# Three couples of tiles in seven products, for the last four attention pairs of layer A

## The chip, the cores and the metric

One Trainium2 chip, and one core of it. The metric is device time of one launch in microseconds; the median of three runs of the kernel before is 2052.78 us (2052.01 to 2052.95).

## What is computed

Two transformer layers over 256 rows of width 2048, in float32. The change touches the first sublayer of layer A, its attention with a combined projection to queries, keys, values and a forget gate:

```
u = rms_norm(h, a_norm_g[l])
proj = u @ a_w_in[l]
q, k, v, fz = jnp.split(proj, [D, 2 * D, 3 * D], axis=-1)
q = rms_norm(q.reshape(B, S, H, Dh), a_q_g[l])
k = rms_norm(k.reshape(B, S, H, Dh), a_k_g[l])
...
o = forgetting_attention(q, k, v, logf)
h = h + o.reshape(B, S, D) @ a_w_out[l]
h = h + sq_relu_mlp(h, mlp_norm_g[layer], mlp_w1[layer], mlp_w2[layer])
```

The rest is an MLP of width 8192, a shared key and value projection, a second attention with a query projection of its own, and a second MLP. All the matrices are 2048 deep or 2048 wide; their float32 weights are read from HBM once, some tiles twice.

## The kernel before

**Products.** A product of 256 rows with a weight is cut into panels of 512 output columns. The rows are two blocks of 128, and the depth is 16 tiles of 128. A *unit* is a weight tile of 128 partitions by 1024 columns: two depth tiles of one panel. Each float32 operand is split in two parts, `hi` (rounded to the format that TensorE multiplies fast) and `lo` (the rest), and a product is three passes: hi times hi (L592), lo of the activations (L594) and lo of the weights (L596). A plain unit is 2 depth tiles x 2 row blocks x 3 passes = 12 matmuls of 512 columns.

**Splitting.** `issue` (L305) takes the next unit: ScalarE (ACT) writes `hi` (L323), VectorE (DVE) subtracts to get `lo` (L324). There are three buffers for each, and `top_up` (L340) keeps up to three units ready ahead of TensorE (PE). `load` (L289) brings plain units into four `raw` buffers from the queue of SyncE (SP), three units ahead (`EARLY`).

**Seven products.** Panels are taken in *pairs* (class `Pair`). Of a pair, the first depth tiles of both panels are multiplied by the scheme of Strassen in Winograd's form: a couple of row blocks, two depth halves and two panels make eight block products, of which seven are needed. One *couple* is such a square of 2 depth tiles x 2 panels. The weights of a pair come as four blocks "11", "12", "21", "22" (`bring`, L921), and the weight side needs the sums T3 = 22 + 12, T2 = T3 + 11, T1 = 12 + 11 and T4 = 21 + T2 (the minus signs lie with the activations), of which T3 and T2 are added by DVE (`make`, L944), and T1 and T4 by an accumulating DMA from GpSimd's (POOL's) queue (`put`, L972), which reads the block a second time. The seven weight operands are called *forms* (11, T3, T2, T1, 21, T4, 22). The activation side needs sums of the row blocks (`sums`, L386; tiles `S`). In the attention of layer A a pair takes two couples: blocks of 128x1024, seven forms of 2 x 3 = 6 matmuls, then six plain units for each of the two panels. In the MLPs a pair takes four couples (`DEEP`), each block 128x2048 and each form split in two halves.

**Order of the work.** Everything on SP, ACT, DVE and PE runs in the order in which Python wrote it (`keep_order`, L88). `plan_heads` (L261) makes the list of units for the attention of layer A: one pair with the panels of (v0, q1), and four more with (k1, v1), (q2, k2), (v2, q3), (k3, v3). `TABLES["ORD"]` interleaves the forms with plain units; the six numbers of `HF` and `HS` say how many plain units before a pair's first form each block is brought or summed (`prepare`, L982). The steps of attention (softmax, norms, transposes) stand in a queue `fill`; `run` (L998) takes as many of them after each unit as the table `HM` says.

**Space.** Blocks lie in the right halves of the four rooms `k0`, `k1`, `v0`, `v1` (`sub`), whose left halves hold normed keys and values; T3 and T2 lie in a tile of the pool `acts`. Query tiles use the tags `q` and `s` (`scale_q`, L692), two buffers of each. `h` holds the residual rows; they are read in at the start and first changed by the output projection.

## Time and profile before

| | |
|---|---|
| median of three runs | 2052.78 us |
| the profiled execution's own time | 2049.66 us |
| its span (first to last instruction) | 2047.9 us |
| granted TensorE clock | 0.999 |
| PE busy | 2041.1 us, 9062 records |
| DVE busy | 1783.5 us |
| ACT busy | 1403.7 us |
| POOL busy | 245.0 us |
| data moved by DMA | 557.78 MB |

"Busy" is the time in which an engine has at least one instruction under way. PE's instructions overlap (a matmul lasts longer than the distance to the next one), so the distance between starts is what a matmul costs. The four attention pairs that the change concerns lie from about 86 us to about 270 us of the span.

### The profile page before, as it was taken

What the parts mean: (1) busy time and instruction counts of PE and PEld (TensorE: products, weight loads), DVE (VectorE), ACT (ScalarE), POOL (GpSimd) and SP (SyncE); (2) the same over time, 40 slices, a digit from 0 to 9 for tenths busy, and PEclk for the clock granted to TensorE, in tenths of its full rate; (3) what the DMA queues carried; (4) which work ended last, traced back from release to release, by engine and by line L of the source; (5) the groups of instructions that cost most, each with busy time, mean ns of one, the idle gap of its engine ahead of it and who ended that gap; (6) DMA issues with size and microseconds to landing.
All of it is one profiled execution on the core that took longest, in us unless ns stands there. A gap on an engine that the chain in (4) does not pass through costs nothing.

```text
span 2047.9 us, 27097 instructions
## 1 busy us (share of the span) xinstructions
PE 2041.1 (100%) x9062; PEld 1688.5 (82%) x9062; DVE 1783.5 (87%) x2065; ACT 1403.7 (69%) x1805; POOL 245.0 (12%) x351
## 2 busy tenths in 40 slices
PE   9999999999999999999999999999999999999999
PEld 7888888888888888888888888888888888888887
DVE  7788888998898899899988778888988998988996
ACT  7766666677677677677778666667766676776764
POOL 1111110011111102101012111001101111111020
PEclk9999999999999999999999999999999999999999
DMA  8898888998888898898879888888988888888984
GB/s 322 265 298 272 266 280 243 309 278 272 282 262 281 272 293 272 247 292 273 260 242 311 275 254 287 255 264 284 291 291 265 266 270 284 266 284 261 299 259 147
DMA packets 175309, 557.78 MB, mean 272 GB/s; under 512 B 40624, under 2 KB 69184, under 8 KB 152640
## 3 DMA queue, kind: packets, MB, share of 16 engines
q1 hardware_dynamic: 154112, 464.99, 63.9%
q0 software_dynamic: 20768, 90.75, 22.5%
q8 instruction: 71, 1.16, 0.2%
q14 instruction: 70, 0.57, 0.1%
q10 hardware_dynamic: 288, 0.30, 0.1%
HBM read 516.07 MB, written 27.29 MB: 265 GB/s over the span
## 4 chain that ended last, share of the span: by engine, by line
PE 98%; DVE 1%; ACT 1%; issue 0%; DMA 0%; DVEq 0%; ACTq 0%
PE acc L596 23%; PE acc L592 23%; PE acc L594 23%; PE s L592 9%; PE s L594 9%; PE s L596 9%; PE po L729 1%; PE po L766 1%; DVE lo L324 0%; PE po L767 0%; PE po L728 0%; ACT hi L323 0%; DMA gsb<-in_gs 0%; PE pg L868 0%; DVE s L995 0%
## 5 line engine op out<-in xcount | busy, mean ns | idle before, releaser
L324 DVE TENSOR_TENSOR lo<-raw,hi 128x1024 fp32r<-128x1024 f32 (+1 forms) x409 | 493.5, 1211 | 81.5 <-ACT hi L323 77.1
L323 ACT ACTIVATE hi<-raw 128x1024 fp32r<-128x1024 f32 (+1 forms) x409 | 429.5, 1054 | 194.0 <-PE acc L594 123.4
L592 PE MATMUL acc<-hi,act 128*128 128x512 f32 x1774 | 496.3, 393 | 0.7 <-ACT hi L323 0.7
L596 PE MATMUL acc<-lo,act 128*128 128x512 f32 x1774 | 491.1, 390 | 0.7 <-DVE lo L324 0.6
L594 PE MATMUL acc<-hi,act 128*128 128x512 f32 x1774 | 490.7, 389 | 0.0
L596 PEld LDWEIGHTS acc<-lo,act 128*128 128x128 f32 x1774 | 332.5, 188 | 72.1 <-DVE lo L324 3.1
L594 PEld LDWEIGHTS acc<-hi,act 128*128 128x128 f32 x1774 | 333.0, 188 | 70.1 <-DVE act L383 0.5
L592 PEld LDWEIGHTS acc<-hi,act 128*128 128x128 f32 x1774 | 331.2, 188 | 69.6 <-ACT hi L323 2.1
L323 ACT ACTIVATE hi<-w 128x1024 fp32r<-128x1024 f32 x254 | 267.0, 1058 | 124.0 <-PE acc L594 82.7
L324 DVE TENSOR_TENSOR lo<-wT,hi 128x1024 fp32r<-128x1024 f32 x220 | 267.2, 1221 | 66.1 <-ACT hi L323 62.2
L324 DVE TENSOR_TENSOR lo<-w,hi 128x1024 fp32r<-128x1024 f32 x254 | 305.3, 1217 | 14.0 <-ACT hi L323 12.3
L323 ACT ACTIVATE hi<-wT 128x1024 fp32r<-128x1024 f32 x220 | 232.1, 1059 | 102.1 <-PE acc L594 48.5
L592 PE MATMUL s<-hi,act 128*128 128x512 f32 x530 | 146.3, 391 | 0.0
L596 PE MATMUL s<-lo,act 128*128 128x512 f32 x530 | 145.0, 389 | 0.0
L594 PE MATMUL s<-hi,act 128*128 128x512 f32 x530 | 144.8, 388 | 0.0
L466 POOL DMA_DIRECT2D q<-z x192 | 95.7, 510 | 255.1 <-DVE z L440 211.0
L596 PEld LDWEIGHTS s<-lo,act 128*128 128x128 f32 x530 | 99.2, 188 | 20.8 <-DVE lo L324 0.5
L594 PEld LDWEIGHTS s<-hi,act 128*128 128x128 f32 x530 | 99.4, 188 | 20.6
L592 PEld LDWEIGHTS s<-hi,act 128*128 128x128 f32 x530 | 99.1, 188 | 20.2
L592 PE MATMUL s<-hi,S 128*128 128x512 f32 x288 | 89.6, 392 | 0.0
L596 PE MATMUL s<-lo,S 128*128 128x512 f32 x288 | 88.8, 390 | 0.0
L594 PE MATMUL s<-hi,S 128*128 128x512 f32 x288 | 88.7, 389 | 0.0
(217 smaller groups left out, 2284.4 us busy)
## 6 DMA issues: line engine op xcount, KB each, us to landing
raw<-in_w_in SPq DMA_DIRECT2D x75, 512.0 KB, 5.9
w<-in_w2fa SPq DMA_DIRECT2D x32, 1024.0 KB, 6.5
w<-in_w2fb SPq DMA_DIRECT2D x32, 1024.0 KB, 6.2
w<-in_w1fa SPq DMA_DIRECT2D x27, 1024.0 KB, 7.0
w<-in_w1fb SPq DMA_DIRECT2D x27, 1024.0 KB, 7.3
raw<-in_w2sa SPq DMA_DIRECT2D x52, 512.0 KB, 7.0
raw<-in_w2sb SPq DMA_DIRECT2D x50, 512.0 KB, 7.3
raw<-in_w_kv SPq DMA_DIRECT2D x48, 512.0 KB, 5.1
```

Of the source, the lines that this page charges most:

```text
L323: S.activation(hi[:, c], raw[:, c], AF.Copy)
L324: V.tensor_tensor(lo[:, c], raw[:, c], hi[:, c].bitcast(F32), op=ALU.subtract)
L466: (G if i % 2 else SY).dma_start(dst[32 * j : 32 * j + 32, i * n : (i + 1) * n], z[32 * i : 32 * i + 32, j * n : (j + 1) * n])
L592: TE.matmul(ps[:, cols], xh, cut(hi, j), start=first, stop=False, **kw)
L594: TE.matmul(ps[:, cols], xl, cut(hi, j), start=False, stop=False, **kw)
L596: TE.matmul(ps[:, cols], xh, cut(lo, j), start=False, stop=last, **kw)
L729: TE.matmul(s[:, P : 3 * P], q[:, a, P:T], k[:, a], start=True, stop=True)
L766: TE.matmul(po[:, :T], v[:, 0, a * P : (a + 1) * P], pT[:, :2], start=True, stop=False)
```

## The change

The last four attention pairs of layer A take three couples of tiles in seven products, where they took two. A block is now 128x1536: 1024 columns in its room as before, and a quarter block of 128x512 beside it. The quarter blocks of `k0`, `k1` lie in one buffer of the tag `s` and those of `v0`, `v1` in the first 1024 columns of the residual tile `h[0]`, whose rows are read again from the input when the output projection's first pair opens. For the room in tag `s`, all query tiles of this layer use tag `q`. Each form comes as a whole one of 6 matmuls, then a half one (128x512) of 3; five plain units for each panel remain. The halves share the `hi` and `lo` buffers with the whole units and count as units of their own in the three that are kept ready. Sums of T3 and T2 are written as two DVE instructions, the accumulating DMAs of T1 and T4 as two issues. The activation sums of the third couple are made by `sum_third`, in four steps that enter the queue of steps at place 10. The tables `HM`, `HT`, `OFH` and the order "three" are new or other.

```diff
-    "HM": (1, 2, 1, 0, 0, 1, 1, 1, 0, 1, 1, 2, 1, 1, 0, 1, 1, 1, 1, 1, 2, 0, 1, 1, 1, 1, 1, 0, 1, 0, 0, 1, 1, 1, 0, 0, 1, 1, 1, 1, 0, 1, 1, 1, 1, 1,
+    "HM": (1, 2, 1, 0, 0, 1, 1, 1, 0, 1, 1, 2, 1, 1, 0, 1, 1, 1, 1, 0, 1, 2, 0, 1, 1, 0, 1, 1, 0, 1, 0, 1, 0, 0, 1, 0, 1, 1, 0, 0, 0, 1, 1, 0, 1, 1,
...
+    "HT": (7, 8, 1, 5, 4, 3),
-    "OFH": (11, 10, 2, 7, 7, 6),
+    "OFH": (9, 8, 1, 6, 6, 5),
+        "deep0": "a4 F F F b4 a5 a6 a7", "three": "a3 a4 F a5 F a6 b3 a7 F b4"},
+    "X3": 10,
...
+        if three is not None:
+            f, s = three
+            for i in range(f.shape[0] // 4):
+                src = [[None] * 3 + [s[5 * (2 * i + q) + u] for u in range(5)] for q in range(2)]
+                big = {k: f[4 * i + m] for m, k in enumerate(("11", "12", "21", "22"))}
+                j = len(pairs) + 1
+                pairs.append(Pair(big, src, "three", j % 2 == 1, TABLES["HT" if i else "HS"], WIDE))
+                pairs[-1].at = 2 * j
...
-                raw = raw[:, UN:]
+                raw = form.pair.e[form.name] if form.pair.e else raw[:, UN:]
...
-        ready.append((hi, lo, n < UN))
+        ready.append((hi, lo, False))
...
-        tag = "qs"[g // 2]
+        tag = "qs"[g // 2 if layer else 0]
...
+            if p.wide:
+                p.e[name] = beside(p.rooms[name])
+                SY.dma_start(p.e[name], p.big[name][:, UN:])
...
+    def beside(tag):
+        if not aside:
+            aside.extend((qkv.tile([P, UN], F32, name="aside", tag="s", bufs=2), h[0][:, :UN]))
+        i = ("k0", "k1", "v0", "v1").index(tag)
+        return aside[i // 2][:, i % 2 * 512 : i % 2 * 512 + 512]
...
         V.tensor_tensor(d, a, b, op=ALU.add)
+        if e:
+            V.tensor_tensor(*e, op=ALU.add)
...
         G.dma_start(p.t[name][:, cols], p.big[other][:, cols], accum_op=ALU.add)
+        if p.e:
+            G.dma_start(p.e[name], p.big[other][:, UN:], accum_op=ALU.add)
...
+    def sum_third(x, fs):
+        y = wk.tile([P, 512], F32, name="y3", tag="wk").rearrange("p (a t) -> p a t", a=2)
+        for j in range(2):
+            V.tensor_tensor(y[:, j], x[2 * UA + j][:, 0].bitcast(F32), x[2 * UA + j][:, 1].bitcast(F32), op=ALU.add)
+        yield
+        s = qkv.tile([P, UN], F32R, name="S", tag="s", bufs=2)
+        fs.extend(s[:, i * 512 : i * 512 + 512] for i in range(2))
+        yield from sums([[y[:, j : j + 1, b * P : (b + 1) * P] for j in range(2)] for b in range(NB)], fs[2:], 1)
...
+            if p.order == "out0" and three:
+                SY.dma_start(h[0][:, :UN], xr[0][:, :UN])
```

What this moves on PE, at the third couple's first use: the start of the second pair (the first of the four), at its form T3 and what follows. `acc` and `s` are accumulators, `S` the activation sums, `po` the small matmuls of attention. Before:

```order
L592 MATMUL acc<-hi,S 128x512 x2
L594 MATMUL acc<-hi,S 128x512 x2
L596 MATMUL acc<-lo,S 128x512 x2
L592 MATMUL s<-hi,act 128x512 x4
L594 MATMUL s<-hi,act 128x512 x4
L596 MATMUL s<-lo,act 128x512 x4
L728 MATMUL po<-R,q 128x128
L729 MATMUL po<-R,q 128x256
```

And after:

```order
L604 MATMUL acc<-hi,S 128x512 x2
L606 MATMUL acc<-hi,S 128x512 x2
L608 MATMUL acc<-lo,S 128x512 x2
L604 MATMUL acc<-hi,S 128x512
L606 MATMUL acc<-hi,S 128x512
L608 MATMUL acc<-lo,S 128x512
L740 MATMUL po<-R,q 128x128
L741 MATMUL po<-R,q 128x256
L604 MATMUL s<-hi,act 128x512 x4
L606 MATMUL s<-hi,act 128x512 x4
L608 MATMUL s<-lo,act 128x512 x4
```

The form has three more matmuls, and the pair of attention's matmuls that stood behind the plain unit now stands ahead of it; over the whole program PE has 12 matmuls fewer (8922 before, 8910 after).

The same place on DVE. `lo<-wT` is the split of T3 or T2, `wT<-wT,R` the sum for T2; `lo<-raw` splits a plain unit; `row`, `pbuf` and `t` are attention's softmax. Before:

```order
L324 TENSOR_TENSOR lo<-wT_843,hi 128x1024
L970 TENSOR_TENSOR wT_843<-wT_843,R 128x1024
L324 TENSOR_TENSOR lo<-raw,hi 128x1024
L749 RECIPROCAL row<-row 128x2
L751 TENSOR_SCALAR pbuf<-pbuf,row 128x128
L751 TENSOR_SCALAR pbuf<-pbuf,row 128x256
L440 STREAM_TRANSPOSE pbuf<-pbuf 128x3x4x32
L738 SCALAR_TENSOR_TENSOR t<-po,cq,nb 128x128
L740 TENSOR_REDUCE row<-t 128x1
L738 SCALAR_TENSOR_TENSOR t<-po,cq,nb 128x256
L740 TENSOR_REDUCE row<-t 128x1
L324 TENSOR_TENSOR lo<-wT_843,hi 128x1024
```

And after:

```order
L336 TENSOR_TENSOR lo<-wT_857,hi 128x512
L999 TENSOR_TENSOR wT_857<-wT_857,R 128x1024
L1001 TENSOR_TENSOR wT_857<-wT_857,h_90 128x512
L761 RECIPROCAL row<-row 128x2
L763 TENSOR_SCALAR pbuf<-pbuf,row 128x128
L763 TENSOR_SCALAR pbuf<-pbuf,row 128x256
L452 STREAM_TRANSPOSE pbuf<-pbuf 128x3x4x32
L750 SCALAR_TENSOR_TENSOR t<-po,cq,nb 128x128
L752 TENSOR_REDUCE row<-t 128x1
L750 SCALAR_TENSOR_TENSOR t<-po,cq,nb 128x256
L752 TENSOR_REDUCE row<-t 128x1
L336 TENSOR_TENSOR lo<-raw,hi 128x1024
```

Behind the split of T3 there are now the split of its half, a sum of 1024, a sum of 512 and a softmax step ahead of the split of the next plain unit, where before the one sum stood.

More of the change, by code (lines that the diff above doesn't have):

```diff
@@ L337, in half_next @@
         u = raws[0][0] if raws else units[0]
-        return isinstance(u, Form) and u.half and not u.pair.deep
+        return False
     def top_up(ahead=AHEAD, early=EARLY):
@@ L1197, in heads @@
         base = turns[0]
-        last = next(p for p, q, i in plan_h[::-1] if isinstance(p, Pair) and p.order in LAZY[:2])
-        run(plan_h, opener(x, fs, evacs, o, out, base, last, TABLES["XOH"]), TABLES["HM"], plan_a[0][0])
+        last = next(p for p, q, i in plan_h[::-1] if isinstance(p, Pair) and p.order == "three")
+        step3 = steps(lambda: sum_third(x, fs))
+        add_fill([[]] * TABLES["X3"] + [[step3]] * 4)
+        run(plan_h, opener(x, fs, evacs, o, out, base, last, TABLES["XOH"], True), TABLES["HM"], plan_a[0][0])
         halves_of.clear()
```

41 lines of the change are left out of this document (28 added, 13 removed), and 6 rows, old and new, of the table TABLES.

## The prediction

> **What bounds the kernel now.** I read the page's engine shares first, then who waits for whom on PE.
>
> ```profile
> PE 2041.1 (100%) x9062; PEld 1688.5 (82%) x9062; DVE 1783.5 (87%) x2065; ACT 1403.7 (69%) x1805; POOL 245.0 (12%) x351
> PE pt L141 <- DVE mhalf L143: 1.0, 1, 1.0
> PE acc L592 <- ACT hi L323: 0.7, 1, 0.7
> PE acc L596 <- DVE lo L324: 0.6, 1, 0.6
> ```
>
> PE waits visibly only three times, 2.3 us in all. Busy time of PE proves little by itself, since its instructions overlap. So I took starts from PE's order in time, at the pair where the change begins (start, duration, engine and line, operation, count):
>
> ```profile
> 95.36 0.61 PE L596 MATMUL acc<-lo,S 128*128 128x512 f32 x2
> 98.54 0.38 PE L728 MATMUL po<-R,q 128*128 128x128 f32 x2
> 99.00 0.82 PE L592 MATMUL acc<-hi,S 128*128 128x512 f32 x2
> 100.57 1.07 PE L592 MATMUL s<-hi,act 128*128 128x512 f32 x4
> 103.29 0.62 PE L592 MATMUL acc<-hi,S 128*128 128x512 f32 x2
> 106.47 0.50 PE L596 MATMUL acc<-lo,act 128*128 128x512 f32 x1
> ```
>
> The plain unit that starts at 100.57 with the first of its three passes ends where the next form starts, at 103.29: 12 matmuls in 2.72 us, 0.2267 us each, with no gap. PE is the bound, and whatever takes matmuls away is worth their full time unless something else comes late. Who could? The stages of the four pairs, and one of the MLP for comparison (columns: stretch, its length, busy time of PE, weight loads, DVE, ACT, POOL, then clock, DMA share, GB/s):
>
> ```profile
> 86.00:131.00 45.00, 45.00 (x206) 37.28 (x205) 41.30 (x68) 30.78 (x55) 6.12 (x6) 1.00 0.88 284
> 131.00:177.00 46.00, 46.00 (x210) 38.31 (x209) 36.26 (x49) 29.56 (x50) 7.04 (x8) 1.00 0.84 261
> 177.00:222.00 45.00, 45.00 (x206) 37.46 (x205) 36.38 (x50) 29.79 (x53) 7.16 (x8) 1.00 0.93 296
> 222.00:270.00 48.00, 48.00 (x220) 40.00 (x219) 43.31 (x74) 31.54 (x60) 7.27 (x7) 1.00 0.80 246
> 460.00:624.00 164.00, 163.97 (x723) 135.27 (x722) 146.76 (x145) 112.13 (x117) 19.05 (x32) 1.00 0.87 274
> ```
>
> DVE is second. It is idle 3.70, 9.74, 8.62 and 4.69 us in the four pairs, 26.75 together; ACT has 14 to 16 us free in each. The question is whether DVE has room where the new work falls, so here is its order in time around the first of the four pairs (in brackets the idle time before, and its releaser):
>
> ```profile
> 88.35 1.22 DVE L324 TENSOR_TENSOR lo<-raw,hi 128x1024 fp32r<-128x1024 f32 x1
> 89.49 0.35 DVE L738 SCALAR_TENSOR_TENSOR t<-po,cq,nb 128x128 f32<-128x128 f32 x1
> 90.92 1.21 DVE L324 TENSOR_TENSOR lo<-wT,hi 128x1024 fp32r<-128x1024 f32 x1
> 92.17 1.23 DVE L970 TENSOR_TENSOR wT<-wT,R 128x1024 f32<-128x1024 f32 x1
> 93.35 1.23 DVE L324 TENSOR_TENSOR lo<-raw,hi 128x1024 fp32r<-128x1024 f32 x1
> 94.49 0.16 DVE L749 RECIPROCAL row<-row 128x2 f32<-128x2 f32 x1
> 95.77 0.31 DVE L738 SCALAR_TENSOR_TENSOR t<-po,cq,nb 128x128 f32<-128x128 f32 x1
> 97.59 1.23 DVE L324 TENSOR_TENSOR lo<-wT,hi 128x1024 fp32r<-128x1024 f32 x1 [0.35 <-ACT hi L323]
> 99.05 1.22 DVE L324 TENSOR_TENSOR lo<-raw,hi 128x1024 fp32r<-128x1024 f32 x1 [0.23 <-ACT hi L323]
> 100.77 0.70 DVE L1020 SCALAR_TENSOR_TENSOR acc<-acc,p 128x512 f32<-128x512 f32 x1 [0.49 <-PE acc L596]
> 101.38 1.22 DVE L324 TENSOR_TENSOR lo<-R,hi 128x1024 fp32r<-128x1024 f32 x1
> 105.20 1.21 DVE L324 TENSOR_TENSOR lo<-raw,hi 128x1024 fp32r<-128x1024 f32 x1
> ```
>
> Two things are to be seen. DVE's lead over PE varies: the split of T3 ends at 92.13 and PE's third pass of T3 needs it at 95.36, a lead of 3.23 us; the split that begins at 105.20 ends at 106.41 and PE takes it at 106.47, a lead of 0.06. And the split at 88.35 lasts 1.22 us but the next instruction begins 1.14 us after its start: instructions overlap by 0.08, and in a row a split costs 1.14.
>
> **What goes from PE.** Per pair the seven forms grow by 7 x 3 = 21 matmuls and two plain units (24) go: 3 fewer, 12 in the four pairs. 12 x 0.2267 = 2.72 us. This is a gain as long as nothing else is late.
>
> **What comes to DVE and ACT.** Prices, from the groups by shape between 46 and 350 us (mean ns of one behind the comma):
>
> ```profile
> L324 DVE TENSOR_TENSOR lo<-raw,hi 128x1024 fp32r<-128x1024 f32 x79 | 95.2, 1214 | 23.2 <-ACT hi L323 22.9 <-DMA pbuf<-turn 0.2
> L405 DVE TENSOR_TENSOR S<-sum,S 128x512 fp32r<-128x512 f32 x4 | 2.6, 683 | 0.0
> L1126 DVE TENSOR_TENSOR y<-act 128x256 f32<-128x256 f32 x4 | 1.4, 416 | 0.0
> L323 ACT ACTIVATE hi<-raw 128x1024 fp32r<-128x1024 f32 x80 | 84.1, 1060 | 26.0 <-PE acc L594 9.4 <-PE s L594 5.8 <-DMA raw<-in_w_oa 3.6
> L402 ACT ACTIVATE S<-sum 128x512 fp32r<-128x512 f32 x3 | 1.8, 633 | 1.1 <-DVE sum L396 1.1
> ```
>
> No half split is in the trace; the nearest row is the same subtraction on 512 columns, 0.683 us, or 0.60 in a row (0.683 less the overlap). A pair gets seven half splits and two half sums, and loses two splits: 9 x 0.60 - 2 x 1.14 = 3.12 us in a row, 9 x 0.683 - 2 x 1.214 = 3.72 at full length. `sum_third` has two additions of 256, four of 128 (0.31, as the step at 95.77) and one split of 512: 2 x 0.416 + 4 x 0.31 + 0.683 = 2.76, or 2.2 in a row. In all 14.7 to 17.6 us. Room is 26.75 less the 2.72 that PE no longer takes: 24.0. ACT gets 7 x 0.633 - 2 x 1.06 = 2.3 us a pair and has 14 to hide it.
>
> So the total fits; the places are another matter. Take the first pair from the end of T3's split, by the order after. To the second plain unit DVE has: half split 0.60, the sum for T2 1.18 (92.17 to 93.35), its half 0.60, a softmax step 1.28 (94.49 to 95.77), the next 1.43 (89.49 to 90.92), a split 1.14: 6.23 us; then T2's split 1.14, its half 0.60, the two softmax steps again 2.71, an accumulator step 0.61 (100.77 to 101.38), a split 1.14: 6.20. Together 12.4. PE, from T3's third pass to the third pass of that second unit: 0.45 of T3, three half matmuls 0.68, attention's pair 0.46 (98.54 to 99.00), a unit 2.72, T2 with its half 2.04, two passes 1.81: 8.16, and some 0.2 because a matmul behind attention's starts late (99.00 takes 0.82 where others take 0.62). DVE falls back by 4.1 on a lead of 3.23: PE waits about 0.8. In the trace DVE also lost 0.35 + 0.23 + 0.49 = 1.07 here to waits, which may or may not vanish when it runs late: 0.8 to 1.9, I take **1.5**. Behind it the queue of DVE holds the other splits, and PE waits for all of them.
>
> The second and third pair have 9.74 and 8.62 free against 3.1 to 3.7: 0 to 0.6 by the same bunching, I take **0.3** for both. The fourth has 4.69 - 0.68 = 4.0 for 3.1 to 3.7, with no reserve for bunching: 0 to 2, I take **0.8**. The sum of waits is 2.6 us, between 0.8 and 4.5.
>
> By the Trainium skill, page "VectorE: DVE Perf Modes", section "The DRAIN you can't avoid", the next op starts only when the pipeline is empty, though the section points to a later one by which an op that isn't held starts earlier. Under the strict reading the new work costs its full length, 17.6 us instead of 14.7. This trace sides with the later one: 1.14 against 1.22.
>
> **Transfers.** Per pair four quarter loads of 256 KB come and two units of 512 KB go, which balance; two accumulating quarters are new, and `h[0]` is read once more.
>
> ```profile
> L980 POOL DMA_DIRECT2D wT<-in_w_in x4 | 3.5, 880 | 46.5 <-DVE lo L324 46.5
> SPq L942 <- DVE lo L324: 3.4, 3, 1.9
> ```
>
> Each accumulation keeps POOL 0.88 us, eight more are 7.0 us, where POOL is busy 6 to 7 us of every 45; the norms' powers queue behind them on POOL, the turns of queries and keys wait for those. SP waits at block loads for a split that frees the room, three times, 1.9 us at most, and the unit loads stand behind; the four buffers and the three ready units, over 5 us of PE's time, cover that. I cost transfers at nothing; if the cover fails, rival C. The reread is one transfer of 512 KB, and a whole pair of the output projection passes before anyone adds to `h[0]`. The third group's queries now wait in tag `q` for the first group's, whose products were done a pair earlier: nothing, and ACT's splits behind them lose nothing. Eight unit loads fewer shift by three places which of every five loads in the MLPs goes to tag `z`; the stages there have PE busy 163.97 of 164 us with one such pattern, and I expect the same of another: nothing either way, at most the 0.7 us of a wait like PE's longest for ACT.
>
> **Sum.** 2049.66 - 2.72 + 2.6 = 2049.5 for the profiled execution; the median of the timed runs stands 3.1 above that execution, and I keep that distance: 2052.78 - 0.1 = **2052.7**. About 0.2%, 4.1 us, is what a measurement of this kernel can tell from no change.
>
> **Forecast (45%).** DVE gives back most of what PE saves: waits of 0.8 to 4.5 us, so 2050.9 to 2054.6.
>
> **Rival A (30%): the whole gain.** The steps of attention lie so that DVE catches up; waits below 0.8, 2050.1 to 2050.9. For it: the MLP stage runs DVE 146.76 of 164 us with PE busy 163.97; before, leads of 0.06 cost nothing. Against it: the fall-back of 4.1 us above.
>
> **Rival B (13%): slower, DVE is full.** Each half split finds its `hi` not ready, since ACT gets one more instruction of fixed cost each time. At the 0.23 us that the row of 99.05 shows, plus the 0.08 of overlap lost, 28 halves cost 8.7 us more: 14.7 + 8.7 = 23.4 of the 24.0 us of room, and every bunch becomes a wait: 2.6 + 0.8 x 8.7 = 9.6 us if a fifth of it still finds idle time; 2052.78 - 2.72 + 9.6 = 2059.7. It decides once waits pass 6.8 us (2.72 + 4.1). By the strict rule of the skill's page the mechanism is the same with 2.9 us in place of 8.7, which would stay within 0.2%.
>
> **Rival C (8%): accumulated quarters land late.** T4's quarter is issued 0.88 us behind its block. If it and T1's hold up their halves by that in all four pairs, and no lead is left, 8 x 0.88 = 7.0, half of it hidden: 2052.7 + 3.5 = 2056.2.
>
> **Rival D (4%): faster by over 0.2%.** Besides 2.72 us the waits at the seam to the MLP would have to go, 0.7 + 0.6: 4.0, and still something from attention's late starts; about 2048.5.
>
> **Range and chances.** From 2050.0 to 2057.0 it takes in the forecast, A and C and leaves out B and D. Faster by over 0.2%: 0.05; within: 0.80 (forecast, A, C less their tails); slower: 0.15 (B and a tail of C).
>
> **What would show it.** PE should have 12 matmuls less; half splits should take about 0.68 us; PE should wait for `lo` in the first and the fourth of the four pairs, 1 to 2 us and about 1; nothing should change in the MLPs. I am wrong if PE waits for `hi` or a DMA there, if the waits lie in the second or third pair, or if the halves leave no trace on PE at all (A).

## The result, and the profile after

The changed kernel takes 2073.94 us, median of four runs (2072.26 to 2077.18); the kernel before took 2052.40 beside it (four runs, 2051.11 to 2052.95). The ratio is 1.011 (95% interval 1.0094 to 1.0126): 21.5 us slower, far outside the range of the prediction. The profiled execution took 2075.57 us, its span is 2073.8.

The page of after (busy time, share of the span, instructions):

```profile
PE 2050.0 (99%) x9050; PEld 1685.6 (81%) x9050; DVE 1799.2 (87%) x2100; ACT 1411.3 (68%) x1826; POOL 255.3 (12%) x359
```

PE has the 12 matmuls fewer. DVE grew by 15.7 us and ACT by 7.6. Who waits, from the waits of PE between 86 and 312 us (us in total, times, longest):

```profile
PE s L604 <- ACT hi L335: 6.6, 4, 3.7
PE acc L604 <- ACT hi L335: 4.3, 5, 1.6
PE acc L608 <- DVE lo L336: 2.6, 5, 1.1
PE s L608 <- DVE lo L336: 1.1, 1, 1.1
```

The first surprise: 10.9 us of waits are for `hi`, ACT's part of a split, and only 3.7 for `lo`, DVE's. And the stages of the pairs, in the stretches that the prediction showed of before:

```profile
86.00:131.00 45.00, 42.93 (x192) 34.55 (x191) 37.76 (x65) 28.32 (x54) 5.13 (x5) 1.00 0.79 235
131.00:177.00 46.00, 43.73 (x194) 35.44 (x194) 38.38 (x52) 32.13 (x52) 7.75 (x8) 1.00 0.91 288
177.00:222.00 45.00, 42.37 (x186) 33.42 (x185) 38.38 (x63) 29.36 (x57) 12.02 (x11) 1.00 0.93 274
222.00:270.00 48.00, 44.61 (x198) 35.91 (x197) 39.12 (x58) 27.43 (x48) 7.25 (x7) 1.00 0.82 247
```

PE is idle 2.1, 2.3, 2.6 and 3.4 us in them, where it had not been idle at all, and yet DVE is idle 6.6 to 8.9 us in each and ACT 14 to 21: nobody is full. That points to an order and not to an amount of work.

For the size of it I add up PE's **gaps**: the distance between the starts of successive matmuls, less what one takes without a gap (0.2267 us at 512 columns, as in the prediction, 0.113 and 0.110 at 256 and 128), from the same matmul to the same matmul (89.2 to 290.4 us in before, 90.1 to 310.6 in after). The stretch takes 201.1 us before and 220.5 after. Its gaps are 5.9 us before (attention's late starts, none over 0.25) and 28.0 after: 22.1 more, which less the 2.72 that the matmuls save makes the 19.4 between the two lengths. 18.1 us of them lie in 18 gaps of over 0.25 us: 4.0 us in the first pair (up to 140 us), 4.8 in the second and third, 9.3 behind 240 us. The rest of the program is 6.5 us longer in this execution, 2.3 and 1.6 of it in the two MLPs, 0.9 ahead of the pairs.

**One of the regular gaps.** ACT in after, at the first of the four pairs (start, duration, operation, in brackets the idle time before and its releaser):

```profile
94.95 0.61 ACT L335 ACTIVATE hi<-wT 128x512 fp32r<-128x512 f32 x1
98.25 0.60 ACT L1051 ACTIVATE p<-acc 128x512 f32<-128x512 f32 x1 [2.68 <-PE acc L608]
98.74 1.05 ACT L335 ACTIVATE hi<-raw 128x1024 fp32r<-128x1024 f32 x1
```

and PE at the same place:

```profile
97.82 0.39 PE L608 MATMUL acc<-lo,S 128*128 128x512 f32 x1
98.05 0.38 PE L740 MATMUL po<-R,q 128*128 128x128 f32 x2
98.27 0.60 PE L741 MATMUL po<-R,q 128*128 128x256 f32 x2
99.84 1.20 PE L604 MATMUL s<-hi,act 128*128 128x512 f32 x4 [0.98 <-ACT hi L335]
```

ACT splits the half of T3, then stands still for 2.68 us until PE has finished that half, copies the product (`p`, line 1051), and only then splits the next plain unit, for which PE waits. In before, the same stretch of ACT:

```profile
92.27 1.04 ACT L323 ACTIVATE hi<-raw 128x1024 fp32r<-128x1024 f32 x1
96.02 0.60 ACT L1015 ACTIVATE p<-acc 128x512 f32<-128x512 f32 x1 [2.70 <-PE acc L596]
```

The copy waits as long, but the split stands ahead of it. That is written in `run`: a form is taken from `ready` without filling it up, and the filling comes behind the copy. In before a plain unit was left in `ready` then. In after the whole form and its half have used up the list.

**The longest gap.** ACT in after, in the last pair:

```profile
282.57 0.38 ACT L782 ACTIVATE act<-po 128x256 fp32r<-128x256 f32 x1 [3.22 <-PE po L779]
283.49 1.15 ACT L414 ACTIVATE S<-sum 128x512 fp32r<-128x512 f32 x2 [0.54 <-DVE row L761]
285.20 1.15 ACT L707 ACTIVATE q<-z,gqk 128x1024 f32<-128x1024 f32 x1 [0.56 <-DMA z<-turn]
286.25 1.06 ACT L672 ACTIVATE sq<-acc 128x512 f32<-128x512 f32 x2
287.21 1.05 ACT L335 ACTIVATE hi<-raw 128x1024 fp32r<-128x1024 f32 x1
```

Four steps, one of them waiting for PE (3.22 us) and one for a turned tile, stand ahead of the split at 287.21, and PE idles 3.72 us. Behind it the clock is low (windows: stretch, length, busy time of PE, weight loads, DVE, ACT, POOL, then clock, DMA share, GB/s):

```profile
286.00:290.00 4.00, 1.69 (x7) 1.37 (x8) 3.07 (x6) 4.00 (x9) 2.10 (x2) 0.96 0.58 153
290.00:292.00 2.00, 2.00 (x6) 1.57 (x5) 2.00 (x3) 1.18 (x2) 2.00 (x3) 0.50 0.99 352
292.00:294.00 2.00, 2.00 (x9) 1.65 (x8) 2.00 (x3) 0.37 (x2) 0.47 (x1) 0.73 0.53 158
```

**The queue of SP.** Softmax tiles, queries and keys are turned over DRAM: SP writes a tile out and reads it back in columns, and in its queue the reading back waits until the write has landed. SP's waits for that between 86 and 312 us, before and after:

```profile
SPq L456 <- DMA turn<-pbuf: 14.2, 9, 3.5
SPq L456 <- DMA turn<-z: 1.4, 1, 1.4
```

```profile
SPq L468 <- DMA turn<-pbuf: 36.7, 9, 7.9
SPq L468 <- DMA turn<-z: 17.7, 5, 5.3
```

16 us became 54. All that time the loads of raw units stand behind it.

So there were three theories. **Late split**, widened to **lead in units**: the list counts a half, 0.68 us of PE, like a plain unit of 2.72, so that whatever on ACT or DVE waits for PE has too little PE work behind it as cover. **Steps and turns**: the new places of attention's steps and SP's waits make tiles and raw units late. **More work**, the prediction's own: DVE and ACT have too much to do.

### The profile page after: what moved, and what is told of

It reads as the page before. It is cut to its first block, busy times and chain, and to the rows that moved or that the text cites. A ratio compares the mean times of both kernels' runs of the same rounds, so it can differ in the third digit from the quotient of the medians.

```text
span 2073.8 us, 27179 instructions
## 1 busy us (share of the span) xinstructions
PE 2050.0 (99%) x9050; PEld 1685.6 (81%) x9050; DVE 1799.2 (87%) x2100; ACT 1411.3 (68%) x1826; POOL 255.3 (12%) x359
## 4 chain that ended last, share of the span: by engine, by line
PE 84%; DMA 3%; DVE 3%; issue 1%; ACT 1%; SPq 0%; DVEq 0%; POOL 0%; ACTq 0%; POOLq 0%
PE acc L608 20%; PE acc L604 19%; PE acc L606 19%; PE s L608 8%; PE s L604 8%; PE s L606 8%; DVE lo L336 2%; DMA wT<-in_w1fb 1%; DMA q<-z 1%; DMA raw<-in_w_qb 1%; PE po L778 1%; PE po L741 1%; DMA w<-in_w2fa 1%; ACT hi L335 0%; DMA z<-turn 0%
## 5 line engine op out<-in xcount | busy, mean ns | idle before, releaser
L335 ACT ACTIVATE hi<-raw 128x1024 fp32r<-128x1024 f32 (+1 forms) x401 | 420.5, 1053 | 201.6 <-PE acc L606 130.3
L336 DVE TENSOR_TENSOR lo<-raw,hi 128x1024 fp32r<-128x1024 f32 (+1 forms) x401 | 484.7, 1214 | 78.2 <-ACT hi L335 73.9
L336 DVE TENSOR_TENSOR lo<-wT,hi 128x1024 fp32r<-128x1024 f32 (+1 forms) x232 | 274.6, 1194 | 64.8 <-ACT hi L335 59.7
L335 ACT ACTIVATE hi<-wT 128x1024 fp32r<-128x1024 f32 (+1 forms) x232 | 239.0, 1037 | 102.4 <-PE acc L606 50.0
L604 PE MATMUL s<-hi,act 128*128 128x512 f32 (+1 forms) x524 | 145.4, 392 | 6.6 <-ACT hi L335 6.6
L608 PE MATMUL s<-lo,act 128*128 128x512 f32 (+1 forms) x524 | 145.0, 391 | 1.1 <-DVE lo L336 1.1
L606 PE MATMUL s<-hi,act 128*128 128x512 f32 (+1 forms) x524 | 144.0, 390 | 0.0
L606 PEld LDWEIGHTS s<-hi,act 128*128 128x128 f32 x524 | 98.4, 188 | 20.6
L604 PE MATMUL s<-hi,S 128*128 128x512 f32 x296 | 92.2, 390 | 0.0
L606 PE MATMUL s<-hi,S 128*128 128x512 f32 x296 | 91.8, 389 | 0.0
```

Source lines behind the costliest of these rows:

```text
L335: S.activation(hi[:, c], raw[:, c], AF.Copy)
L336: V.tensor_tensor(lo[:, c], raw[:, c], hi[:, c].bitcast(F32), op=ALU.subtract)
L604: TE.matmul(ps[:, cols], xh, cut(hi, j), start=first, stop=False, **kw)
L606: TE.matmul(ps[:, cols], xl, cut(hi, j), start=False, stop=False, **kw)
L608: TE.matmul(ps[:, cols], xh, cut(lo, j), start=False, stop=last, **kw)
```

## The experiments

Each is compared with the kernel before on the same chip. "Gaps" are those of the pairs' stretch in the one profiled execution, less the 5.9 us of before. The kernels named own_ are own_buffers, each with the edit shown.

| kernel | median, us | against before | ratio, 95% interval | gaps, us |
|---|---|---|---|---|
| changed kernel | 2073.94 | +21.5 | 1.0110 (1.0094 to 1.0126) | 22.1 |
| split_first | 2071.37 | +18.5 | 1.0094 (1.0080 to 1.0108) | 20.8 |
| scale_later | 2079.66 | +26.8 | 1.0130 (1.0112 to 1.0147) | 22.6 |
| z_shift | 2072.54 | +20.6 | 1.0095 (1.0081 to 1.0109) | 20.2 |
| after_gap_bias | 2078.99 | +26.9 | 1.0129 (1.0114 to 1.0145) | 28.2 |
| own_buffers | 2068.77 | +16.8 | 1.0080 (1.0067 to 1.0092) | 16.7 |
| own_bias_later | 2068.14 | +16.4 | 1.0078 (1.0065 to 1.0092) | 15.1 |
| own_no_adds | 2064.12 | +12.4 | 1.0060 (1.0048 to 1.0072) | 12.2 |
| own_gap | 2065.53 | +13.8 | 1.0065 (1.0053 to 1.0077) | 11.7 |
| own_gap_bias | 2064.32 | +12.2 | 1.0058 (1.0044 to 1.0072) | 12.0 |
| own_gap_bias_even | 2063.47 | +11.3 | 1.0051 (1.0039 to 1.0064) | 11.3 |
| own_values_later | 2062.30 | +10.9 | 1.0053 (1.0040 to 1.0066) | 8.2 |
| before_late_split | 2063.04 | +10.2 | 1.0057 (1.0043 to 1.0071) | 10.3 |
| before_fewer_places | 2054.47 | +2.7 | 1.0013 (1.0005 to 1.0022) | 2.4 |
| before_more_splits_end | 2054.04 | +2.1 | 1.0006 (0.9997 to 1.0015) | 5.2 |
| before_more_splits | 2099.48 | +46.6 | 1.0231 (1.0217 to 1.0245) | |
| before_gap_behind | 2097.81 | +45.7 | 1.0220 (1.0207 to 1.0234) | |
| before_gap | 2052.00 | 0.0 | 1.0001 (0.9992 to 1.0010) | |
| before_gap_1024 | 2050.76 | -0.7 | 0.9999 (0.9990 to 1.0008) | |

Where the intervals of two rows overlap, their times do not tell them apart. That holds for split_first, scale_later, z_shift and after_gap_bias against the changed kernel, and for own_bias_later, own_no_adds, own_gap and own_gap_bias against own_buffers. Readings of these rest on their traces, one execution each (that of scale_later is the fastest of its four, that of after_gap_bias the slowest).

### The late split, put into before and taken out of after

before_late_split:

```diff
+            n = plan[i + 1] if i + 1 < len(plan) else (p, 0, 0)
+            late = n[0].order == "qkv" and n[0].at >= 4 and n[1:] in ((2, 1), (2, 2))
-            hi, lo = ready.popleft()[:2] if q > 1 and ready and not p.deep else fetch()
+            hi, lo = ready.popleft()[:2] if q > 1 and ready and not p.deep else fetch(AHEAD - late)
```

> The kernel before with one edit: ahead of T3 and of T2 of the last four attention pairs one unit fewer is kept ready, so the plain unit behind each of them is split behind the P7 copy and the accumulator step; every engine's work is that of the kernel before. Theory 'late split': at each of four T3 places PE idles for the P7 copy and the split, 1.1 to 1.8 us as in the changed kernel, and for 0.3 to 1.3 at each T2 place: 6 to 12 us slower, 2058 to 2064. Theories 'more work' and 'steps and turns': neither changes, so within 2 us of the kernel before.

10.2 us slower, as the theory says. What PE waits for in it between 86 and 300 us:

```profile
PE acc L592 <- ACT hi L323: 3.8, 3, 1.6
PE s L592 <- ACT hi L323: 3.3, 2, 1.6
PE acc L596 <- DVE lo L324: 0.6, 1, 0.6
```

The gaps behind the four T3 are 1.79 us each, by the distances; two of after's are the same 1.79. With no half, no added work and no other transfer, the order of one split against one copy makes waits for `hi` of the kind seen in after.

split_first:

```diff
                 form_products(p.ps, hi, lo, p.x, p.fs, u, q == 3, p)
+                if p.order == "three" and q == 2 and u in (1, 2):
+                    top_up(AHEAD - 1)
```

> The changed kernel with one edit: behind the whole form of T3 and of T2 the next plain unit is split at once, so that its hi and lo stand ahead of the P7 copy on ACT and of the accumulator step on DVE; no work is added or taken. Theory 'late split' (with the half as a unit of its own the list of ready units is empty at the half of T3 and of T2, so the next split queues behind steps that wait for PE): the four stalls behind T3's halves (1.24, 1.14, 1.79, 1.79 us, 6.0 together) and those behind T2's halves (1.25, 0.27 and what the others hold) go, 7 to 9 us in all: about 2066, from 2064 to 2068. Theory 'more work' (DVE and ACT have too much to do in the pairs): the work is the same, so 2072 to 2076. Theory 'steps and turns' (attention's steps and the round trips of the turned tiles stand ahead of splits and loads): the stalls move on to the next such place, 2070 to 2075.

ACT now splits ahead of the copy, and two of the four gaps behind T3 are gone; the other two (1.35 us at 99.7, 1.83 at 194.0) are now waits for the `lo` of the same unit, which DVE reaches late. Only 3 us of the 21.5 come back, not 7 to 9, and the intervals overlap. What PE waits for:

```profile
PE po L740 <- DMA R<-turn: 3.8, 1, 3.8
PE s L604 <- ACT hi L335: 3.6, 2, 3.3
PE s L608 <- DVE lo L336: 3.4, 3, 1.7
```

A turned tile is late now, 3.97 us by the distances at 302.2, where the changed kernel lost 0.3. The late split is a cause, and other waits lie close behind it.

### The halves outside the list

own_buffers:

```diff
-        hi = wsp.tile([P, UN], F32R, name="hi", bufs=3)[:, :n]
-        lo = wsp.tile([P, UN], F32R, name="lo", bufs=3)[:, :n]
+        if n < UN:
+            hi, lo = (aside[2][:, i * 512 : i * 512 + 512] for i in range(2))
+        else:
+            hi, lo = (wsp.tile([P, UN], F32R, name=i, bufs=3) for i in ("hi", "lo"))
...
-        ready.append((hi, lo, False))
+        ready.append((hi, lo, n < UN))
...
-        return False
+        return isinstance(u, Form) and u.half and not u.pair.deep
...
-            aside.extend((qkv.tile([P, UN], F32, name="aside", tag="s", bufs=2), h[0][:, :UN]))
+            aside.extend((h[1][:, :UN], h[0][:, :UN], qkv.tile([P, UN], F32R, name="halves", tag="s", bufs=2)))
...
-                SY.dma_start(h[0][:, :UN], xr[0][:, :UN])
+                for b in range(NB):
+                    SY.dma_start(h[b][:, :UN], xr[b][:, :UN])
```

> The changed kernel with one edit: the halves have hi and lo buffers of their own and do not count in the three units that are kept ready, so that the list holds as many whole units as in the kernel before. The room comes from the tag s buffer of the quarter blocks, which move to the first 1024 columns of h[1] and are reread like those of h[0], 512 KB more. The splits and sums on DVE and ACT are those of the changed kernel. Theory 'lead in units' (the list counts a half, 0.68 us of PE, as it counts a plain unit, 2.72, so whatever on ACT or DVE waits for PE has less PE work behind it as cover; the late splits are its sharpest form): most of the 22 us of waits in the four pairs go, 12 to 22 us faster than the changed kernel: 2052 to 2061. Theory 'more work': nothing changes, 2071 to 2076. Theory 'steps and turns': 0 to 5 us faster, the stalls at 284 and 305 us of the span stay.

4.7 us faster than the changed kernel (both against before), not 12 to 22. Up to 260 us the theory holds: gaps of over 0.25 us fall there from 11.4 us to 3.3, and PE hardly waits for splits any more. Behind 260 us it fails, and they rise from 6.7 us to 11.5. What PE waits for:

```profile
PE po L742 <- DMA R<-turn: 5.6, 2, 4.3
PE po L780 <- DMA pbuf<-turn: 4.9, 1, 4.9
```

The first of the two late tiles on SP's queue, and PE's row behind it:

```profile
265.17 1.85 SPq L470 DMA_DIRECT2D z<-turn  x4
267.06 0.43 SPq L464 DMA_DIRECT2D turn<-pbuf  x1
276.42 1.73 SPq L470 DMA_DIRECT2D pbuf<-turn  x4
```

```profile
279.68 1.19 PE L780 MATMUL po<-pbuf,R 128*128 128x256 f32 x2 [4.89 <-DMA pbuf<-turn]
```

The write is issued at 267.06 and the reading back at 276.42. In between SP does nothing: the write of 192 KB takes 8.9 us. Its median in before is 3.6, in after 5.0, here 5.6. Late turned tiles are a second cause, and the next runs look for what makes them late.

### What makes the turned tiles late

own_no_adds:

```diff
-        if p.e:
-            G.dma_start(p.e[name], p.big[other][:, UN:], accum_op=ALU.add)
```

> The kernel with own buffers for the halves, with the accumulating transfers of the quarter blocks for T1 and T4 left out (two of 256 KB in each of the four pairs; the sums T1 and T4 of the third couple are then missing from the result). Theory 'transfers' (the additional traffic of the quarters makes the turned tiles' writes slow, 5.6 us median where before 3.6, and with them the two stalls of 5.05 and 4.45 us at 274 and 298 us): 5 to 10 us faster than with own buffers, 2059 to 2064. Theory 'queue of SP' (SP stands still between the write of a turned tile and its reading back, because the steps lie otherwise): within 2 us of own buffers, 2067 to 2071.

4.4 us faster than own_buffers (both against before), a little less than the theory of transfers says. The writes of softmax tiles in own_buffers, own_no_adds and, further down, own_gap (KB each, median us from issue to landing, 86 to 312 us):

```profile
turn<-pbuf SPq DMA_DIRECT2D x12, 192.0 KB, 5.6
turn<-pbuf SPq DMA_DIRECT2D x14, 192.0 KB, 4.2
turn<-pbuf SPq DMA_DIRECT2D x14, 192.0 KB, 3.7
```

The accumulating quarters cost something, and their own halves are not late: no split waits for them. That they slow the tiles beside them fits the first two medians, but it is not shown. The third, with the quarters in place, is lower still; and of the two long stalls the one at 274 us fell from 5.05 to 2.62, while the one at 298 became 5.36.

own_gap:

```diff
-        st["carry"] = carry(z, st["pT"], 0)
+        st["carry"] = carry(z, st["pT"], 1 if cq is not None else 0)
```

> The kernel with own buffers, with one more step between the write of a turned softmax tile and its reading back, in layer A; the step that uses the tile stays. Theory 'queue of SP': SP's waits for those writes (44.4 us between 80 and 310 us of the span, 14.2 in the kernel before) fall below 25, the raw loads behind them come earlier and ACT's waits for them (8.9 us) go, PE gains 1 to 4 us: 2065 to 2068; but the tile is read back a step later, and where a value step comes soon behind it the stall stays. Theory 'transfers': the tile comes later, same or 1 to 5 us slower.

3.0 us faster than own_buffers. SP's waits for the writes of softmax tiles fall from 44.4 to 16.6 us (86 to 312 us), those for the other writes from 20.9 to 11.6:

```profile
SPq L470 <- DMA turn<-pbuf: 16.6, 5, 5.8
SPq L470 <- DMA turn<-z: 11.6, 4, 4.8
```

The late tile at 298 us is gone. One long wait is left, at 266 us, 5.84 us by the distances:

```profile
PE po L780 <- DMA pbuf<-turn: 5.7, 1, 5.7
```

own_bias_later, and own_gap_bias with the gap as well:

```diff
-        for i in (5, 8, 9) if cq and g == 0 else (3, 6, 7):
+        for i in (5, 8, 9) if cq and g in (0, 3) else (3, 6, 7):
```

> The kernel with own buffers, with the three steps of the last group's bias (a transfer of 768 KB on POOL's queue, 0.4 us behind the write of a turned tile that then took 8.9 us, and two selects) two places later. Theory 'collision' (the bias transfer and the turned tile's write share the DMA engines, and the stall of 5.05 us at 274 and the low clock behind it come from that): 4 to 8 us faster than own buffers, 2061 to 2065. Theory 'queue of SP' or 'transfers': within 2 us of own buffers.

> Own buffers for the halves, the longer gap between a turned softmax tile's write and its reading back, and the last group's bias two places later, all three. With the gap alone one long stall was left in the pairs, 5.84 us at 266 us behind a reading back that was issued with the bias transfer; the later bias alone had taken 3.1 us from the stall at 274. Theory 'collision': the stall falls by 3 us or more and the low clock behind it goes: 2058 to 2062, against 2065.5 with the gap alone. Theory 'closeness of the steps': the tile is issued too late in any case, 2064 to 2067.

The bias alone brings 0.4 us against before, within the intervals; the gap at 274 us fell from 5.05 to 1.93, but the one at 298 rose from 4.45 to 5.24 and one at 156 from 1.5 to 2.9. With the longer gap it brings 1.6, within the intervals as well, and the long wait falls from 5.84 to 4.55. The time lies in the window that the theory gave for the closeness of the steps: of the time, the collision with the bias is a small part at most.

own_gap_bias_even (from own_gap_bias), where the places 105 to 109 of `HM` in the last pair change, and own_values_later (from that):

```diff
-0, 2, 0, 0, 2
+1, 1, 0, 1, 1
```

```diff
-    "ATA": ((10, 13, 15, 19, 9), (9, 12, 15, 18, 12), (8, 13, 15, 19, 9), (9, 9, 12, 12, 9)),
+    "ATA": ((10, 13, 15, 19, 9), (9, 12, 15, 18, 12), (8, 13, 15, 19, 11), (9, 9, 12, 12, 9)),
```

> As own_gap_bias, and in the last pair the two places where two steps follow each other (behind a5 and a6) are spread: one of each two is taken a half unit earlier, behind the half form. Theory 'closeness of the steps': a stall that is left in the last pair falls by 2 us or more against own_gap_bias, 2 to 4 us faster than it. Theory 'collision': within 1.5 us of it.

> As own_gap_bias_even, and the third group's four value steps (a product on PE that reads a turned tile, and a split on ACT and DVE that waits for it) come two places later. If their places make the waits that are left in the last pair (2.03 us at 258 us with 0.45 and 0.39 behind it), these go: 2 to 4 us faster than own_gap_bias_even, 2059 to 2062. If not, within 1.5 us of 2063.5, and what is left lies in the tiles' way itself.

Each brings less than the theory asked: 0.9 and 0.4 us against before, inside the intervals. The gaps show more than the times do. The wait of 4.55 us at 269 is gone in the first, with 2.03 new at 258 and 1.33 at 296. In the second the gaps are 3.1 us shorter, and no gap is left over 2 us. The intervals do not carry these steps one by one, nor the 2.9 us that they and own_gap_bias bring together against own_gap. The whole way from own_buffers to own_values_later, 5.9 us, they do carry.

after_gap_bias, the same two edits without own buffers:

> The changed kernel with the gap and the later bias, and the halves still counted as units. If the ready list and the turned tiles are separate causes, the gain against the changed kernel is that of own_gap_bias against own buffers: 6 to 10 us, 2064 to 2068. If the turned tiles stall PE only where the ready list is full (or if the late splits cover those stalls), less than 3 us, 2071 or more.

It is 5.3 us above the changed kernel (both against before), which the intervals do not tell from no change, and not 6 to 10 below it. Its trace has a wait of 5.49 us at 281 for a turned tile and the gaps behind T3 as well. So the two repairs do not simply add. That reading a tile back later helps only where PE has units ready while it waits would explain it, but is not shown.

### The steps and the work by themselves, in the kernel before

before_fewer_places:

```diff
+                if p.order == "qkv" and p.at >= 4 and q < 2 and u == 2:
+                    masks[i + 1] += masks[i]
+                    masks[i] = 0
```

> The kernel before with one edit: in the last four attention pairs no step of attention is taken after the two plain units that the change removes (a2 and b2); their steps are taken after the next item, so that a pair has 17 places for its steps in place of 19, as in the changed kernel, and at two of them two steps follow each other. Work, units and transfers stay. Theory 'fewer places' (the steps stand closer, so that between the parts of one step's chain, a turned tile's write and its reading back above all, less time passes): 5 to 12 us slower than before, with stalls at turned tiles. Theories 'transfers' and 'lead in units': within 2 us of the kernel before.

2.7 us slower: a real cost, but below the 5 to 12 of the theory, and the gaps are in four places of 0.4 to 0.6 us.

before_more_splits and before_more_splits_end, which differ only in where the buffer `hih` lies:

```diff
+        if form and form.pair.order == "qkv" and form.pair.at >= 4:
+            hih = wsp.tile([P, 416], F32R, name="hih", bufs=1)
+            S.activation(hih, raw[:, :416], AF.Copy)
+            V.tensor_tensor(hih, raw[:, :416], hih.bitcast(F32), op=ALU.subtract)
```

```diff
+    last_pool = pool("more", 1)
...
-            hih = wsp.tile([P, 416], F32R, name="hih", bufs=1)
+            hih = last_pool.tile([P, 416], F32R, name="hih", bufs=1)
```

> The kernel before with one addition: each of the seven forms of the last four attention pairs gets a second split of 416 columns whose result nobody reads (28 ACT copies, 28 DVE subtractions). At 0.58 us, or 0.50 in a row, that is 3.5 to 4.1 us of DVE in each pair, about the 3.1 to 3.7 net that the change adds, and 3.9 us of ACT where the change adds 2.3. The order of the units and the number ready stay. Theory 'more work': most of the 22 us of waits come back, 10 to 20 us slower; by the prediction's own terms 1 to 5 slower. Theories 'late split' and 'steps and turns': below 2 us.

> The kernel with the 28 second splits again, but their buffer of 1664 bytes lies in a pool behind all others, where it lay in front of all pools but the first; the same instructions on the same engines. In the last run PE's matmuls followed each other at 0.2326 us in place of 0.2267 throughout the program, and the four pairs took 205.1 us in place of 200.0, hardly more than that pace explains (4.9). If the shift of every later tile's address by 1664 bytes did it, this kernel is within 3 us of the kernel before, and 'more work' is worth at most that. If the splits themselves did it, it is again 40 to 50 us slower.

The first cost 46.6 us, but nearly all of it outside the pairs, from a slower pace of every matmul that has nothing to do with the work (last section). The second is the clean one: 2.1 us by the medians, interval of the ratio 0.9997 to 1.0015, with the added splits at full price:

```profile
L330 DVE TENSOR_TENSOR hih<-R,hih 128x416 fp32r<-128x416 f32 x16 | 9.8, 612 | 0.0
L330 DVE TENSOR_TENSOR hih<-wT,hih 128x416 fp32r<-128x416 f32 x12 | 7.0, 585 | 0.0
L329 ACT ACTIVATE hih<-R 128x416 fp32r<-128x416 f32 x16 | 8.7, 542 | 0.0
```

They add 16.8 us of DVE, about as much as the change does. Its trace, an execution 3 us above the median, shows 5.2 us of gaps, 2.8 of them at two turned tiles behind 280 us. "More work" is worth 3 us at most by the interval, about what the prediction gave it, and no 22.

### Two smaller edits

scale_later (the last group's scaling of queries four places later) and z_shift (the counter of the MLPs' loads starts at 8):

```diff
-                    add_fill([[]] * (7 + (0 if g else 6)) + [[lambda: qs.update({g: scale_q(box[1], 0, g)})]])
+                    add_fill([[]] * (7 + (4 if g == 3 else 0 if g else 6)) + [[lambda: qs.update({g: scale_q(box[1], 0, g)})]])
...
-    extra = [False, 0]
+    extra = [False, 8]
```

> The changed kernel with one edit: the last group's scaling of queries, an ACT step that waits for the turned tile's landing at 285.09 us, comes four places later in the queue of steps. Theory 'steps and turns': PE's longest idle stretch (3.88 us at 284.2) loses the 1.15 us of the step and the 0.56 of its wait, and with them what follows of the low granted clock (0.50 at 290 to 292, some 2 us): 2 to 4 us faster, 2070 to 2072. Theories 'late split' and 'more work': the stall stays in another place, within 1 us of the changed kernel.

> The changed kernel with one edit: the counter that sends every fifth load of the MLPs to tag z starts at 8, so that the same loads go there as in the kernel before. Theory 'z pattern' (the 2.3 us and 1.6 us that the two MLPs lose in the trace of after come from other loads in the two z buffers): 2 to 4 us faster, 2070 to 2072. Otherwise within 1 us of the changed kernel, and the MLPs' waits come from something else.

scale_later is not faster (2073.38 to 2083.52, the widest of all). The gap at 284 us fell from 3.88 to 2.17, and one of 3.12 us appeared at 305 for a turned tile: handed on again. By its time z_shift is the changed kernel within its spread: in its trace the first MLP lost 0.7 us against before instead of 2.3, the second 3.0 instead of 1.6. But one place can be told. From the same matmul to the same, 812 to 926 us in before and in the first MLP, the eleven other traces of changed kernels take 1.2 to 2.9 us longer than that of before. That of z_shift takes 0.01 longer, and those of before_gap, before_gap_1024, before_fewer_places, before_late_split and before_more_splits_end at most 0.03. Each of the eleven has a gap of 0.7 to 1.4 us at one matmul there, which none of the others has. In after it is this one:

```profile
944.30 0.74 PE L604 MATMUL acc<-hi,act 128*128 128x512 f32 x2 [0.68 <-ACT hi L335]
```

So the shifted pattern of tag `z` costs the changed kernel about 1 us there. In the second MLP it does not show.

## Why the prediction was wrong

- **12 matmuls fewer, 2.72 us**: right; PE has 9050 records for 9062, and they have the price of 0.2267 us wherever nothing is late.
- **The price and sum of the new work**: right. A half split takes 0.682 us on DVE and 0.624 on ACT (0.68 and 0.633 were forecast):

```profile
L336 DVE TENSOR_TENSOR lo<-wT,hi 128x512 fp32r<-128x512 f32 x12 | 8.2, 682 | 1.8 <-ACT hi L335 1.8
L335 ACT ACTIVATE hi<-wT 128x512 fp32r<-128x512 f32 x12 | 7.5, 624 | 0.0
```

  DVE's busy time rose 15.7 us, within the 14.7 to 17.6. As much work added to before cost 2.1 us, close to the 2.6 of waits in the sum.
- **The step that failed: ACT's part put at nothing, since ACT "has 14 to hide it"**, and with it the cover, "the four buffers and the three ready units, over 5 us of PE's time, cover that". The cover was claimed for loads behind SP's waits, but the same list hides a late split. I counted the list in units, and the change makes some units four times shorter: behind T3 it held 2.04 us of PE (a form and its half) and then nothing. I followed DVE instruction by instruction through the first pair, and never ACT. There the copy behind T3's half stood ahead of a split, as ACT's order after shows; in before this and T2's place cost 10.2 us when only the order is changed. Free time on ACT did not help: it idled 2.68 us in front of the copy, in order. In the changed kernel itself, own_buffers takes the halves out of the list, and nearly all waits for splits go; of the time 4.7 us come back, since the turned tiles then cost more.
- **Where the waits lie**: 1.5 us was forecast for the first pair, 0.3 for the second and third and 0.8 for the fourth, all for `lo`. The gaps were 4.0, 4.8 and 9.3, mostly for `hi`. The prediction named both signs by which it would be wrong, waits for `hi` and waits in the second and third pair.
- **Transfers at nothing**: wrong. Rival C named the accumulating quarters, and nearly their price (3.5 us; leaving them out of own_buffers brought 4.4, with some 3.6 either way, an estimate from the two intervals), which is luck: it was not their own halves that were late. What was late are the turned tiles, and SP's queue behind them; how much of that the quarters cause is open. I wrote that the turns wait for POOL, and did not ask what stands behind a turn on SP.
- **Rival B** had the sign, and named ACT's `hi`, but not the mechanism. It priced the half splits' waits for their own `hi` at 8.7 us; in the row above they are 1.8 for twelve of the 28 halves, and the other sixteen waited for none. DVE was never full, and PE waited for the `hi` of the unit behind the half.
- **The steps' new places** I did not price. They cost 2.7 us in before. The longest gap in after has four steps ahead of the split, and a low clock behind it; moving one of them (scale_later) only handed the wait on.
- **Nothing changes in the MLPs**: wrong for the first. The shifted pattern of tag `z`, put at nothing or at most 0.7 us, costs about 1 us at one place (z_shift). The rest is not settled: the trace of after has 2.3 and 1.6 us more in the two MLPs, other kernels with the units of before up to 1.8 and 2.1 more in theirs, so part lies in the single execution. But over all that stands behind the pairs' stretch, the twelve traces of changed kernels are 3.5 to 7.6 us longer than that of before, and the five named under z_shift only 0.9 to 2.6.

The parts, each taken by itself in before or on own buffers: -2.72 (matmuls) + 10.2 (late split) + 2.7 (fewer places) + 2.1 (work) + 4.4 (accumulating quarters) = 16.7 of the 21.5 us. That they can be added is not shown, and the runs speak against it: the late split is 10.2 put into before, but own_buffers brings 4.7 back, and the two repairs of after_gap_bias bring nothing. From the other side, the edits from own_buffers to own_values_later took 10.6 us of the loss back and left 10.9: 8.2 us of gaps in the pairs less 2.72, and some 5 in the rest of the program, of which the last bullet explains about 1. None of the variants beats the kernel before.

## What to carry to other kernels

A look-ahead counted in units is worth what its shortest units cover: when a change cuts a unit, recount the lead in microseconds of the bound engine at each place where another engine waits for it. In an engine that runs in order, idle time is no reserve: look for the instruction that waits, and for what stands behind it, on each engine and on the DMA queue, before counting its busy share. And a stall that is taken away may only uncover the next one, so expect less than its length back and measure repairs together as well as singly.

## What the runs showed of the hardware

**The place of a buffer sets the pace of the matmuls.** before_gap_behind adds to before only an unused buffer of 1664 bytes (and one clearing of it), behind the three `hi` and three `lo` buffers and ahead of all other tiles:

```diff
+        if not gap:
+            gap.append(wsp.tile([P, 416], F32R, name="gap", bufs=1))
+            G.memset(gap[0].bitcast(F32), 0.0)
```

> The kernel before with an unused buffer of 1664 bytes in the first pool, taken behind the hi and lo buffers (in before_gap it was taken ahead of them): hi and lo keep their addresses and all other tiles move by 1664 bytes, as in the first kernel with second splits. If the distance between the weights' buffers and the other tiles sets the pace of the matmuls, PE's matmuls follow each other at 0.2326 us again and the time is 2093 to 2102. If not, 2050 to 2054, and that run's pace stays unexplained.

> The kernel before with no work added but an unused buffer of 1664 bytes in the first pool (one clearing of it at the start), which moves every later tile by as much. If the addresses set the pace of the matmuls, 40 to 50 us slower, 2093 to 2102; if not, the same as before.

> As before_gap_behind, with an unused buffer of 1024 bytes in place of 1664. If the pace depends on the distance between the weights' buffers and the other tiles at a grain of 1024 bytes or more, again slower (2070 to 2105); if 1024 is a multiple of the grain, 2050 to 2054 with matmuls 0.2267 us apart.

It costs 45.7 us. Two successive passes of a plain unit in it, and in before_gap_1024:

```profile
611.11 1.10 PE L595 MATMUL acc<-hi,act 128*128 128x512 f32 x4
612.05 1.10 PE L597 MATMUL acc<-hi,act 128*128 128x512 f32 x4
```

```profile
608.42 1.07 PE L595 MATMUL s<-hi,act 128*128 128x512 f32 x4
609.33 1.07 PE L597 MATMUL s<-hi,act 128*128 128x512 f32 x4
```

Four matmuls take 0.94 us there and 0.91 here; over some 2,100 of them between 500 and 1000 us the mean is 0.2333 against 0.2267. In a stretch of the MLP the windows show fewer matmuls at the same busy time and the same clock, 705 for 723:

```profile
460.00:624.00 164.00, 164.00 (x705) 131.93 (x704) 145.36 (x143) 109.69 (x115) 18.18 (x31) 1.00 0.86 270
```

In before_gap the same 1664 bytes lie ahead of `hi` and `lo` too, so that everything moves together, and in before_gap_1024 the distance grows by 1024 bytes: both cost nothing. So it is the distance between the weights' buffers and the tiles behind them that counts, not the addresses, and not every distance (the places follow from the order in which the kernel takes its tiles; the trace does not hold them). Which pair of tiles it is, and at what grain, was not tried. By the Trainium skill, page "SBUF — State Buffer", section "Who interferes with whom", PE never waits on anyone; as far as that means that PE's pace doesn't depend on where its operands lie, these runs differ, and the measurement decides. An experiment that adds a buffer should be checked for it, by PE's pace in a stretch that it doesn't touch: without before_more_splits_end the first run would have been read as proof of "more work".

**The clock after a pause.** Behind PE's pause of 3.72 us in after the clock was 0.50 for the two microseconds from 290, and behind 4.89 us in own_buffers 0.50 from 278 to 282. The 12 matmuls from 288.31 on in after take 4.17 us instead of 2.72, so the pause costs 1.45 us more than its length. The Trainium skill, page "TensorE: Matmul & The Clock Gate", section "Part 1: The HAM clock gate", says that the clock falls to half after an idle window of about 3.4 us; these traces agree with that only in part. Pauses of 2.46 us (own_no_adds, 272 us) and 3.05 us (z_shift, 283 us) left the clock at 1.00, but one of 1.86 us in own_gap_bias_even, from 259 to 260.6, was followed by 0.50 from 263 to 265. So the length of a pause alone does not tell whether the clock falls.
